# A Strassen SwiGLU stage in a fixed order: VectorE one product behind ScalarE, pair ends inside the next pair, two products in a PSUM bank of their own

## The chip, the cores and the metric

One core of a Trainium2 chip runs the whole layer. Times are device microseconds of that core for one execution; the kernel before takes 1094.98 us, the median of three runs (1094.83 to 1096.09).

## The reference

A bidirectional encoder layer on x (1 x 512 x 1024, float32): a half-step SwiGLU feed-forward net, a token mixer (a Fourier branch and multi-head latent attention, gated and summed), a second half-step SwiGLU net and a final norm. Each sub-layer starts with an RMS norm with a shift and a scale from the conditioning vector. The change lies in the second feed-forward net:

```python
def swiglu(h, w_gate, w_up, w_down):
    return (jax.nn.silu(h @ w_gate) * (h @ w_up)) @ w_down

h = modulate(rms_norm(x, ffn2_norm[l]), sh3, sc3)
x = x + 0.5 * g3[:, None, :] * swiglu(h, ffn2_w_gate[l], ffn2_w_up[l], ffn2_w_down[l])
```

D_MODEL is 1024, D_FF 2816, that is 22 hidden tiles of 128 rows.

## The kernel before

Activations lie channel-major: 128 channels by 512 tokens. Float32 operands are split in two parts in the matmul's own format: `hi` is a cast on ScalarE (L94 for weights, L108 for activations), `lo` a subtraction on VectorE (L95, L108) of `hi` from the raw tile. Three matmuls, `hi*hi`, `hi*lo` and `lo*hi` (L103 to L105), make one product of 128 channels. So every weight tile costs a load on SP's queue, a cast and a subtraction before TensorE can use it.

The second feed-forward net (`ffn_pairs`) works on pairs of hidden tiles. The first pair is computed plainly, into four banks (`out`). The other ten are Strassen pairs (class `Pair`): with the two hidden tiles, two halves of the channels and two halves of the tokens as the two-by-two blocks, each of the two weights (gate, up) needs seven products of 128 x 256 for each 512 channels, named after the block of h they take: "21", "11", "t1", "t2", "t3", "t4" and "22". A product is four chunks of three matmuls, 12 in all, of 256 columns. `Pair.run` writes out the 14 products with the sums, silus and multiplies around them; the loops go over u = 0 (gate) and u = 1 (up). In it

- `R1[u]` is a bank with "21" in its lower half and "11", later "t2", "t3" and "t4" added on, in its upper half; `R2[u]` takes "t1" and "22". All come from six banks in turn (`pbank()`); a pool `aux` of two more banks serves the norms.
- after "11", ScalarE copies the upper half to E1 (L451) and VectorE adds the lower half to it (L452).
- `release()` takes the next item off `feed.todo`: a cast and a subtraction of a weight tile that a later product needs, ending in `feed.load`, which issues the next load on SP (and, for the sum of two weight blocks, a second load on POOL's queue that adds in memory, L405). VectorE makes the other sums of blocks (L419, L420). There are six buffers each for `hi` and `lo`, five for raw tiles.
- at the end of a pair come the two hidden tiles: `second` and `s`, each a cast and a subtraction, `s` last, after the last product.

The pairs come in parts of 3, 3, 3 and 2 pairs, the plain pair being in the first part; after each part but the last, eight down projections of 128 x 512 use its hidden tiles, the last two in the order `second`, `s` (L562 adds the result to x). The first Strassen pair also has the two hidden tiles of the plain pair to finish (`aside`, L517 and L518). Inside `manual_schedule` every engine runs its instructions in the order in which the code issues them; what waits for what follows from the tiles and, in PSUM, from whole banks.

Of the kernel before, what the change touches and what calls it, by code (L numbers as in the profile page):

```python
# [10 lines left out]
F32 = mybir.dt.float32  # L11
# [49 lines left out]
def encoder_layer(ctx: ExitStack, tc: tile.TileContext, a: dict):  # L61
# [284 lines left out]
    class Feed:  # L346
# [3 lines left out]
        def __init__(self, ahead, sums_ahead):  # L350
            self.todo, self.raws, self.doubled = [], [], []
            self.ahead, self.sums_ahead = ahead, sums_ahead
# [10 lines left out]
        def release(self):  # L363
            if self.todo:
                self.todo.pop(0)()

    class Unit:
# [12 lines left out]
        def make(self):  # L380
            self.w = split(self.raw, self.n * len(self.src))
            self.feed.load(1)

    class Pair:


        def __init__(self, feed, ws, i):
            self.feed, self.ws, self.i = feed, ws, i
            self.sums, self.first, self.a1, self.s31, self.s24 = [], [], [], [], []
            self.E1, self.E2, self.R1, self.R2, self.summed = [], [], [], [], [False, False]  # L390
            for u in range(2):
                feed.doubled.append(lambda u=u: self.load_sum(u))
                feed.raws.append(lambda u=u: self.load_first(u))
                feed.todo.append(lambda u=u: self.a1.append(split(self.first[u], D)))
            feed.raws.append(self.load_last)
            for u in range(2):
                feed.todo.append(lambda u=u: self.s31.append(split(self.sums[u], D)))
                feed.todo.append(lambda u=u: self.make_s24(u))
# [24 lines left out]
        def make_s24(self, u):  # L423
            self.sum(u)
            self.s24.append(split(self.first[u], D))
            self.feed.load(1, 1)

        def make_a22(self):
            self.a22 = split(self.last, D)
            self.feed.load(1)  # L430
# [6 lines left out]
        def run(self, following=None, aside=()):  # L437

            aside = list(aside)
            V, A, release = nc.vector, nc.scalar, self.feed.release  # L440
            lo, hi = slice(0, HALF), slice(HALF, S)
            for u in range(2):
                R1 = pbank()
                self.R1.append(R1)
                self.product(R1[:, lo], self.a1[u], 1, "21", True)
                if aside:
                    aside.pop(0)()
                self.product(R1[:, hi], self.a1[u], 0, "11", True)
                E1 = tmp.tile([P, S], F32, tag=("sg", "t")[u], name=nm("E1"))
                self.E1.append(E1)  # L450
                A.copy(E1[:, lo], R1[:, hi])  # L451
                V.tensor_add(E1[:, lo], R1[:, lo], E1[:, lo])  # L452
                if u == 0:
                    A.activation(E1[:, lo], E1[:, lo], AF.Silu)
                release()
            g, up = self.E1
            for u in range(2):
                R2 = pbank()
                self.R2.append(R2)
                self.product(R2[:, lo], self.s31[u], 1, "t1", True)  # L460
                if u == 0:
                    V.tensor_mul(g[:, lo], up[:, lo], g[:, lo])
                self.product(self.R1[u][:, hi], self.s24[u], 0, "t2", False)
                A.copy(self.E1[u][:, hi], self.R1[u][:, hi])
                if u == 0 and following is not None:
                    following.sum(0)
            for u in range(2):
                self.product(self.R1[u][:, hi], self.s31[u], 0, "t3", False)
                E2 = tmp.tile([P, HALF], F32, tag=("sq", "ssum")[u], name=nm("E2"))
                self.E2.append(E2)  # L470
                A.copy(E2, self.R1[u][:, hi])
                V.tensor_add(E2, self.R2[u][:, lo], E2)
                if u == 0:
                    A.activation(E2, E2, AF.Silu, scale=-1.0)
                release()

            sg = slot32()[:, 0]
            self.product(self.R1[0][:, hi], self.a22, 0, "t4", False)
            V.scalar_tensor_tensor(sg[:, hi], self.E2[1], -1.0, self.E2[0], op0=ALU.mult, op1=ALU.mult)
            A.activation(sg[:, lo], self.R1[0][:, hi], AF.Silu, scale=-1.0)  # L480
            if following is not None:
                following.sum(1)
            self.product(self.R1[1][:, hi], self.a22, 1, "t4", False)
            V.scalar_tensor_tensor(sg[:, lo], self.R1[1][:, hi], -1.0, sg[:, lo], op0=ALU.mult, op1=ALU.mult)
            release()
            self.product(self.R2[0][:, lo], self.s24[0], 1, "22", False)
            V.tensor_add(g[:, hi], self.R2[0][:, lo], g[:, hi])
            A.activation(g[:, hi], g[:, hi], AF.Silu)
            second = slot()
            split_to(second[:, 0], second[:, 1], sg)  # L490
            release()
            self.product(self.R2[1][:, lo], self.s24[1], 1, "22", False)
# [4 lines left out]
            release()  # L497
            return [s, second]

    def ffn_pairs(ws, wd, gk, early, whole, after):  # L500
# [43 lines left out]
        following = next(pairs)  # L544
        with tc.manual_schedule(engines={E.DVE, E.Activation, E.PE, E.SP, E.Pool}):
            for pi, nk in enumerate(PARTS):
                last = pi == len(PARTS) - 1
                for n in range(1 if pi == 0 else 0, nk // 2):
                    pr, following = following, next(pairs, None)
                    got = pr.run(following if n + 1 < nk // 2 else None,  # L550
                                 [lambda j=j: hidden(*out[2 * j:2 * j + 2]) for j in range(2)] if pr is early else ())
# [653 lines left out]
```

## Time and profile before

| | |
|---|---|
| median of three runs | 1094.98 us (1094.83 to 1096.09) |
| profiled execution, its own time | 1094.74 us |
| its span, first to last instruction | 1093.0 us |
| TensorE busy | 1056.8 us, 97% |
| VectorE busy | 697.7 us, 64% |
| ScalarE busy | 453.8 us, 42% |
| stage of the Strassen pairs and their down projections | about 740 to 1058 us of the span |

PE is TensorE, PEld its weight loads, DVE VectorE, ACT ScalarE, POOL GpSimd, SP the queue that issues most loads. L103 is line 103 of the kernel; the helpers that all stages use have one line each, so tiles tell more than lines. Matmuls overlap, and their ends are modelled: a difference between two starts is safer than an idle time. A wait is put down to the instruction that ended last before it.

### The profile page before, as it was taken

The page shows a single profiled execution, that of the slowest core. Times are in us where ns is not written, and L with a number is a line of the kernel's source. Part 1 is how long each engine was busy: PE and PEld are TensorE (multiplying, and loading weights), DVE is VectorE, ACT ScalarE, POOL GpSimd, SP SyncE. Part 2 cuts the span into 40 slices and gives each one's busy share as a digit, 9 for nine tenths or more (in the row PEclk, how much of TensorE's full clock was granted, in tenths as well). Part 3 has the DMA queues.
Part 4 walks back from the last instruction along what each step waited for, and adds up shares of the span by engine and source line. Part 5 has one row for each costly group of instructions (what it writes and reads, how often), then busy time and mean ns, then how long its engine had stood idle before and what let it go on. Part 6 is the DMA issues. An engine that isn't in the chain of part 4 may idle for free.

```text
span 1093.0 us, 15644 instructions
## 1 busy us (share of the span) xinstructions
PE 1056.8 (97%) x6040; PEld 924.5 (85%) x6040; DVE 697.7 (64%) x1201; ACT 453.8 (42%) x761; POOL 104.4 (10%) x122
## 2 busy tenths in 40 slices
PE   5999999999999999999999989998999999999996
PEld 3888888888888998888888878998889888998996
DVE  6976645862563689752167767797656756665665
ACT  5532222222222444442267664365424533552454
POOL 1000000000000001000145444001000000000000
PEclk9999999999999999999999999999999999999998
DMA  9885642762473156541121124617625663573112
GB/s 360 328 316 162 232 146 87 224 216 80 143 242 97 59 199 219 176 142 39 39 66 52 58 96 128 210 40 203 195 73 159 145 211 84 157 171 110 60 38 78
DMA packets 60044, 159.61 MB, mean 146 GB/s; under 512 B 6129, under 2 KB 9841, under 8 KB 59970
## 3 DMA queue, kind: packets, MB, share of 16 engines
q1 hardware_dynamic: 55250, 143.08, 39.5%
q0 software_dynamic: 4144, 15.01, 6.5%
q8 instruction: 47, 0.77, 0.3%
q10 hardware_dynamic: 576, 0.52, 0.1%
q14 instruction: 27, 0.22, 0.1%
HBM read 154.40 MB, written 4.19 MB: 145 GB/s over the span
## 4 chain that ended last, share of the span: by engine, by line
PE 78%; DVE 8%; ACT 5%; issue 4%; DMA 2%; POOL 2%; SPq 0%; POOLq 0%; DVEq 0%; ACTq 0%
PE ps_mm L103 24%; PE ps_mm L104 24%; PE ps_mm L105 23%; PE ps_mm L590 3%; DVE lo L95 2%; ACT hi L94 2%; ACT f L108 2%; PE ps_mm L978 1%; PE ps_aux L970 1%; POOL yb L1055 1%; DMA raw<-in_wg 1%; DMA g<-in_xtok 1%; DMA g<-in_wg 1%; DVE f L108 1%; PE ps_aux L160 1%
## 5 line engine op out<-in xcount | busy, mean ns | idle before, releaser
L104 PE MATMUL ps_mm<-f,hi 128*128 128x512 f32 (+1 forms) x1120 | 408.3, 365 | 0.7 <-DVE f L108 0.7
L103 PE MATMUL ps_mm<-f,hi 128*128 128x512 f32 (+1 forms) x1120 | 408.2, 366 | 0.0
L105 PE MATMUL ps_mm<-f,lo 128*128 128x512 f32 (+1 forms) x1120 | 407.3, 364 | 0.0
L94 ACT CAST hi<-raw 128x1024 fp32r<-128x1024 f32 (+4 forms) x217 | 198.2, 916 | 363.7 <-PE ps_mm L104 283.8
L95 DVE TENSOR_TENSOR lo<-raw,hi 128x1024 fp32r<-128x1024 f32 (+3 forms) x205 | 225.4, 1101 | 140.4 <-ACT hi L94 138.7
L104 PEld LDWEIGHTS ps_mm<-f,hi 128*128 128x128 f32 x1120 | 211.2, 189 | 34.8 <-DVE f L108 1.6
L103 PEld LDWEIGHTS ps_mm<-f,hi 128*128 128x128 f32 x1120 | 210.6, 189 | 34.4 <-ACT f L108 1.7
L105 PEld LDWEIGHTS ps_mm<-f,lo 128*128 128x128 f32 x1120 | 211.0, 189 | 33.2
L103 PE MATMUL ps_mm<-b,hi 128*128 128x256 f32 x624 | 178.1, 286 | 10.4 <-DVE E L452 10.4
L104 PE MATMUL ps_mm<-b,hi 128*128 128x256 f32 x624 | 177.3, 284 | 0.0
L105 PE MATMUL ps_mm<-b,lo 128*128 128x256 f32 x624 | 177.1, 284 | 0.0
L103 PEld LDWEIGHTS ps_mm<-b,hi 128*128 128x128 f32 x624 | 120.1, 193 | 12.4 <-DVE E L452 12.0
L104 PEld LDWEIGHTS ps_mm<-b,hi 128*128 128x128 f32 x624 | 120.3, 193 | 0.1
L105 PEld LDWEIGHTS ps_mm<-b,lo 128*128 128x128 f32 x624 | 120.3, 193 | 0.0
L133 DVE SCALAR_TENSOR_TENSOR raw<-raw,g 128x1024 f32<-128x1024 f32 x56 | 68.3, 1221 | 32.5 <-DMA raw<-in_ada_w 32.2
L152 POOL TENSOR_TENSOR r<-ms,nhalf 128x2 f32<-128x2 f32 x10 | 9.5, 956 | 398.6 <-DVE ms L150 398.6
L248 DVE TENSOR_TENSOR sg<-ps_mm,sg 128x512 f32<-128x512 f32 x22 | 15.1, 690 | 50.6 <-PE ps_mm L105 50.4
L562 DVE SCALAR_TENSOR_TENSOR g<-ps_mm,gate,g 128x512 f32<-128x512 f32 x24 | 18.0, 749 | 37.7 <-PE ps_mm L105 37.7
L95 DVE TENSOR_TENSOR lo<-g,hi 128x1024 fp32r<-128x1024 f32 (+1 forms) x28 | 32.0, 1144 | 2.0 <-ACT hi L94 1.8
L94 ACT CAST hi<-g 128x1024 fp32r<-128x1024 f32 (+1 forms) x28 | 27.7, 988 | 13.3 <-PE ps_mm L104 11.6
L958 ACT ACTIVATE g<-ps_mm,st 128x512 f32<-128x512 f32 x32 | 22.1, 691 | 19.5 <-DVE st L957 17.2
L590 PE MATMUL ps_mm<-f,hi 128*128 128x512 f32 x96 | 26.3, 413 | 0.7 <-ACT f L210 0.7
(190 smaller groups left out, 1041.9 us busy)
## 6 DMA issues: line engine op xcount, KB each, us to landing
raw<-in_ada_w SPq DMA_DIRECT2D x56, 512.0 KB, 4.3
raw<-in_wd SPq DMA_DIRECT2D x48, 384.0 KB, 3.6
raw<-in_wu SPq DMA_DIRECT2D x35, 512.0 KB, 4.1
raw<-in_wg SPq DMA_DIRECT2D x31, 512.0 KB, 4.3
raw<-in_win SPq DMA_DIRECT2D x21, 512.0 KB, 3.5
g<-in_ada_w SPq DMA_DIRECT2D x16, 512.0 KB, 9.3
g<-in_wg SPq DMA_DIRECT2D x10, 512.0 KB, 5.0
g<-in_wg POOLq DMA_DIRECT2D x10, 512.0 KB, 6.3
```

The lines of the kernel that those rows point to most:

```text
L94: nc.scalar.copy(hi[:, :n], raw[:, :n])
L95: engine.tensor_sub(lo[:, :n], raw[:, :n], hi[:, :n].bitcast(F32))
L103: nc.tensor.matmul(out, lhsT=lh, rhs=rh, start=first, stop=False, skip_group_check=onto)
L104: nc.tensor.matmul(out, lhsT=lh, rhs=rl, start=False, stop=False, skip_group_check=onto)
L105: nc.tensor.matmul(out, lhsT=ll, rhs=rh, start=False, stop=last, skip_group_check=onto)
L108: return nc.scalar.copy(hi, src), engine.tensor_sub(lo, src, hi.bitcast(F32))
L133: nc.vector.scalar_tensor_tensor(raw, raw, 1.0, cb.rearrange("p c t -> p (c t)"), op0=ALU.mult, op1=ALU.mult, accum_out=mod[:, j:j + 1])
L160: nc.tensor.matmul(R[:, lo:lo + HALF], lhsT=ones, rhs=dg, start=True, stop=True)
L248: nc.vector.tensor_mul(sg, pu, sg)
L562: nc.vector.scalar_tensor_tensor(xs(m), po, gate[gk][:, m:m + 1], xs(m), op0=ALU.mult, op1=ALU.add)
L590: nc.tensor.matmul(out[i], lhsT=w[:, i * P:(i + 1) * P], rhs=h1[c][:, part], start=c == 0 and w is wh and part == 0, stop=c == NC - 1 and ...
L958: nc.scalar.activation(pr, sc, AF.Exp, bias=st[:, c:c + 1], accum_out=st[:, 4 + c:5 + c])
```

## The change

1. **A bank for the two "21" products.** `Q` comes from the `aux` banks; "21" of the gate goes to its lower, "21" of the up weight to its upper half. `R1[u]` keeps its upper half alone.
2. **Subtractions one product behind their casts.** `Feed.cut` issues the cast and queues the subtraction (and the load behind it) in `feed.low`; `cast()` takes the next cast, `rest()` the next subtraction, and `run` has both written in at fixed places. The `lo` tile of a new weight thus comes later than its `hi`.
3. **Pair ends inside the next pair.** A pair that has a follower in its part returns `end` (the last add, the multiply and the cast of hidden tile `first`) and `low` (its subtraction). The next pair runs them after its first and second product. A pair without a follower runs them itself, with no prefetch cast between.
4. The silus, sums, copies and `aside` steps are set into new places between the products; `aside` comes after the second and the fourth product instead of after the first and the third.

The core of the diff:

```diff
+        def cast(self):
+            if self.todo:
+                self.todo.pop(0)()
+        def rest(self):
+            if self.low:
+                self.low.pop(0)()
+        def cut(self, raw, n, then=lambda: None):
...
+            nc.scalar.copy(hi[:, :n], raw[:, :n])
+            def low():
+                nc.vector.tensor_sub(lo[:, :n], raw[:, :n], hi[:, :n].bitcast(F32))
+                then()
+            self.low.append(low)
+            return hi, lo
...
-            self.s24.append(split(self.first[u], D))
-            self.feed.load(1, 1)
+            self.s24.append(self.feed.cut(self.first[u], D, lambda: self.feed.load(1, 1)))
...
-        def run(self, following=None, aside=()):
+        def run(self, following, late=(), aside=()):
...
+            Q = pbank("aux", 2)
+            R1, R2 = [pbank() for _ in range(2)], []
...
+            self.product(Q[:, lo], self.a1[0], 1, "21", True)
+            late_step()
+            self.product(R1[0][:, hi], self.a1[0], 0, "11", True)
+            A.copy(g[:, lo], R1[0][:, hi])
+            feed.cast()
+            late_step()
+            if late_given:
+                feed.rest()
+            aside_step()
+            self.product(Q[:, hi], self.a1[1], 1, "21", True)
+            V.tensor_add(g[:, lo], Q[:, lo], g[:, lo])
+            feed.rest()
+            self.product(R1[1][:, hi], self.a1[1], 0, "11", True)
+            A.copy(up[:, lo], R1[1][:, hi])
+            A.activation(g[:, lo], g[:, lo], AF.Silu)
+            feed.cast()
+            aside_step()
+            R2.append(pbank())
+            self.product(R2[0][:, lo], self.s31[0], 1, "t1", True)
...
+            self.product(R1[0][:, hi], self.s31[0], 0, "t3", False)
+            A.copy(E2[0], R1[0][:, hi])
+            feed.cast()
+            self.product(R1[1][:, hi], self.s31[1], 0, "t3", False)
+            A.copy(E2[1], R1[1][:, hi])
+            feed.cast()
+            V.tensor_add(E2[0], R2[0][:, lo], E2[0])
+            feed.rest()
...
-            V.tensor_add(up[:, hi], self.R2[1][:, lo], up[:, hi])
-            V.tensor_mul(g[:, hi], up[:, hi], g[:, hi])
-            s = slot()
-            split_to(s[:, 0], s[:, 1], g)
-            release()
-            return [s, second]
+            def end():
+                V.tensor_add(up[:, hi], R2[1][:, lo], up[:, hi])
+                V.tensor_mul(g[:, hi], up[:, hi], g[:, hi])
+                A.copy(first[:, 0], g)
+            def low():
+                V.tensor_sub(first[:, 1], g, first[:, 0].bitcast(F32))
+            if following is None:
+                end()
+                low()
+                feed.rest()
+                feed.release()
+                return [first, second], ()
+            return [first, second], (end, low)
```

How it moves the instructions, at three places. Names of tiles carry their numbers; `b_1134` is block "t2" of h, `b_1132` block "t1", `b_1077` block "21" and `b_1071` block "11".

**TensorE in the second pair of the second part, from "t1" to "t2" of the gate weight**, with what an instruction waits for. Before, the target `ps_mm_1289` is R1 of the gate:

```order
L103 MATMUL ps_mm_1298_7612<-b_1132_6504,hi_1274_7454 128x256
L104 MATMUL ps_mm_1298_7612<-b_1133_6505,hi_1274_7454 128x256
L105 MATMUL ps_mm_1298_7612<-b_1132_6504,lo_1275_7455 128x256
L103 MATMUL ps_mm_1289_7545<-b_1134_6509,hi_1277_7488 128x256 [waits DVE_49]
L104 MATMUL ps_mm_1289_7545<-b_1135_6510,hi_1277_7488 128x256
L105 MATMUL ps_mm_1289_7545<-b_1134_6509,lo_1278_7489 128x256
```

Now the target is `ps_mm_1291`, again R1 of the gate:

```order
L103 MATMUL ps_mm_1302_7614<-b_1132_6504,hi_1277_7453 128x256
L104 MATMUL ps_mm_1302_7614<-b_1133_6505,hi_1277_7453 128x256
L105 MATMUL ps_mm_1302_7614<-b_1132_6504,lo_1278_7454 128x256
L103 MATMUL ps_mm_1291_7539<-b_1134_6509,hi_1280_7489 128x256 [waits Activation_49]
L104 MATMUL ps_mm_1291_7539<-b_1135_6510,hi_1280_7489 128x256
L105 MATMUL ps_mm_1291_7539<-b_1134_6509,lo_1281_7490 128x256 [waits DVE_49]
```

The matmul that opens "t2" waited for VectorE and now waits for ScalarE; the third one, which takes the low part of the weight, now has a wait for VectorE. Three products earlier, "21" of the up weight begins in the upper half of the new bank (`ps_aux_1290`), without a wait at its first matmul:

```order
L103 MATMUL ps_mm_1291_7539<-b_1071_6048,hi_1269_7362 128x256
L104 MATMUL ps_mm_1291_7539<-b_1072_6049,hi_1269_7362 128x256
L105 MATMUL ps_mm_1291_7539<-b_1071_6048,lo_1270_7363 128x256
L103 MATMUL ps_aux_1290_7538<-b_1077_6070,hi_1275_7437 128x256
L104 MATMUL ps_aux_1290_7538<-b_1078_6071,hi_1275_7437 128x256
```

**ScalarE where the same pair begins.** Before, E1_1260 is the last hidden tile of the pair ahead, E1_1290 the first of this one, `hi` a weight:

```order
L488 ACTIVATE E1_1260_7322<-E1_1260_7322 128x256
L108 CAST f_1281_7512<-g_1276_7458 128x512
L94 CAST hi_1282_7515<-g_1196_6837 128x1024
L108 CAST f_1284_7533<-E1_1260_7322 128x512
L94 CAST hi_1285_7536<-raw_1236_7136 128x1024
L451 COPY E1_1290_7570<-ps_mm_1289_7545 128x256
L454 ACTIVATE E1_1290_7570<-E1_1290_7570 128x256
L94 CAST hi_1291_7574<-raw_1249_7236 128x1024
```

Now (E1_1264 and E1_1293):

```order
L379 CAST hi_1282_7505<-g_1204_6871 128x1024
L532 CAST f_1286_7516<-g_1279_7458 128x512
L534 ACTIVATE E1_1264_7302<-E1_1264_7302 128x256
L379 CAST hi_1288_7533<-raw_1238_7138 128x1024
L543 CAST f_1287_7517<-E1_1264_7302 128x512
L478 COPY E1_1293_7541<-ps_mm_1291_7539 128x256
L379 CAST hi_1295_7571<-raw_1251_7238 128x1024
L488 COPY E1_1294_7542<-ps_mm_1292_7540 128x256
```

The last hidden tile's cast (`f_1284`, now `f_1287`) was followed by a weight's cast and then by the copy of "11"; now the copy follows it at once, and the weight's cast stands before it.

**ScalarE where the first Strassen pair begins.** `ps_mm_1128` is a bank of the plain pair, `b` are blocks of h. Before:

```order
L94 CAST hi_1149_6544<-raw_1140_6523 128x1024
L517 ACT_TABLE_LOAD
L517 ACTIVATE sg_1164_6594<-ps_mm_1128_6307 128x512
L94 CAST hi_1151_6548<-g_1045_5894 128x1024
L108 CAST b_1134_6509<-w_1046_5897 128x1024
L108 CAST b_1136_6514<-w_1048_5899 128x1024
L108 CAST b_1138_6519<-w_1047_5898 128x1024
L94 CAST hi_1153_6554<-raw_1141_6525 128x1024
L108 CAST f_1165_6597<-sg_1164_6594 128x512
L451 COPY E1_1166_6612<-ps_mm_1163_6581 128x256
```

Now:

```order
L379 CAST hi_1149_6544<-raw_1140_6523 128x1024
L379 CAST hi_1151_6548<-g_1045_5894 128x1024
L108 CAST b_1134_6509<-w_1046_5897 128x1024
L108 CAST b_1136_6514<-w_1048_5899 128x1024
L108 CAST b_1138_6519<-w_1047_5898 128x1024
L478 COPY E1_1166_6584<-ps_mm_1164_6582 128x256
L379 CAST hi_1153_6554<-raw_1141_6525 128x1024
L379 CAST hi_1168_6611<-raw_1142_6527 128x1024
L573 ACT_TABLE_LOAD
L573 ACTIVATE sg_1170_6614<-ps_mm_1128_6307 128x512
```

The table load and the silu of the plain pair's first hidden tile stood ahead of the casts of the blocks of h and now stand behind two weight casts that follow them.

## Rows read from the trace of the kernel before

**Rows 1.** Page, part 1: busy time, share of the span, instructions of each engine.

```profile
PE 1056.8 (97%) x6040; PEld 924.5 (85%) x6040; DVE 697.7 (64%) x1201; ACT 453.8 (42%) x761; POOL 104.4 (10%) x122
```

**Rows 2.** Waits (who waited for whom: us, times, longest), 742 to 1058, and after 760.

```profile
PE ps_mm L103 <- DVE E L452: 10.4, 8, 1.8
...
DVE raw L419 <- DMA g<-in_wg: 1.7, 1, 1.7
...
PE ps_mm L104 <- DVE f L108: 0.7, 3, 0.2
...
PE ps_mm L103 <- DVE E L452: 7.4, 6, 1.3
```

**Rows 3.** Windows: stretch and us, busy (xinstructions) of PE, PEld, DVE, ACT, POOL, clock, DMA, GB/s.

```profile
787.80:821.27 33.47, 33.24 (x147) 26.97 (x145) 18.21 (x22) 9.39 (x11) 0.00 (x0) 1.00 0.36 122
821.27:885.03 63.76, 61.24 (x506) 60.68 (x505) 42.50 (x63) 31.10 (x55) 5.17 (x6) 1.00 0.65 167
...
1015.66:1057.61 41.95, 40.69 (x338) 40.48 (x337) 27.60 (x40) 20.12 (x34) 0.00 (x0) 1.00 0.16 51
```

**Rows 4.** Timeline of PE around one wait: start, us, what [idle before <-releaser].

```profile
848.38 0.28 PE L104 MATMUL ps_mm<-b,hi 128*128 128x256 f32 x1
848.50 0.28 PE L105 MATMUL ps_mm<-b,lo 128*128 128x256 f32 x1
850.04 0.38 PE L103 MATMUL ps_mm<-b,hi 128*128 128x256 f32 x1 [1.26 <-DVE E L452]
850.26 0.28 PE L104 MATMUL ps_mm<-b,hi 128*128 128x256 f32 x1
```

**Rows 5.** Timeline of ACT, then of DVE, around the same wait.

```profile
847.35 1.05 ACT L94 CAST hi<-raw 128x1024 fp32r<-128x1024 f32 x1
848.29 0.36 ACT L451 COPY E<-ps_mm 128x256 f32<-128x256 f32 x1
...
848.42 1.23 DVE L95 TENSOR_TENSOR lo<-raw,hi 128x1024 fp32r<-128x1024 f32 x1 [0.26 <-ACT hi L94]
849.57 0.42 DVE L452 TENSOR_TENSOR E<-ps_mm,E 128x256 f32<-128x256 f32 x1
```

**Rows 6.** Timeline of PE, then of DVE, at the end of the last pair of the first part.

```profile
790.77 0.39 PE L104 MATMUL ps_mm<-f,hi 128*128 128x512 f32 x1
791.00 0.39 PE L105 MATMUL ps_mm<-f,lo 128*128 128x512 f32 x1
791.39 0.50 PE L103 MATMUL ps_mm<-f,hi 128*128 128x512 f32 x1
792.12 0.50 PE L104 MATMUL ps_mm<-f,hi 128*128 128x512 f32 x1 [0.23 <-DVE f L108]
...
788.93 0.96 DVE L95 TENSOR_TENSOR lo<-raw,hi 128x768 fp32r<-128x768 f32 x1
789.81 0.42 DVE L493 TENSOR_TENSOR E<-ps_mm,E 128x256 f32<-128x256 f32 x1
...
791.37 0.69 DVE L108 TENSOR_TENSOR f<-E,f 128x512 fp32r<-128x512 f32 x1 [0.69 <-ACT f L108]
```

**Rows 7.** Timeline of PE in the first Strassen pair.

```profile
748.10 0.28 PE L105 MATMUL ps_mm<-b,lo 128*128 128x256 f32 x1
749.55 0.39 PE L103 MATMUL ps_mm<-b,hi 128*128 128x256 f32 x1 [1.17 <-DVE E L452]
...
754.50 0.38 PE L103 MATMUL ps_mm<-b,hi 128*128 128x256 f32 x1 [1.82 <-DVE E L452]
```

**Rows 8.** Timeline of ACT at the start of the first Strassen pair.

```profile
737.12 1.28 ACT L517 ACT_TABLE_LOAD   x1
738.41 0.60 ACT L517 ACTIVATE sg<-ps_mm 128x512 f32<-128x512 f32 x1
...
746.25 1.05 ACT L94 CAST hi<-raw 128x1024 fp32r<-128x1024 f32 x1 [3.46 <-DVE raw L420]
```

**Rows 9.** Windows, columns as in rows 3: the stretch at a lower granted clock.

```profile
755.80:759.20 3.40, 3.40 (x18) 3.40 (x17) 1.70 (x4) 0.56 (x2) 0.00 (x0) 0.50 1.05 220
```

More of the change, by code (lines that the diff above doesn't have):

```diff
@@ L457, in run @@
[L457 to L475, printed above, removed]
@@ new lines, in run @@
+            self.product(R2[0][:, lo], self.s31[0], 1, "t1", True)
+            V.tensor_add(up[:, lo], Q[:, hi], up[:, lo])
+            V.tensor_mul(g[:, lo], up[:, lo], g[:, lo])
+            feed.rest()
+            self.product(R1[0][:, hi], self.s24[0], 0, "t2", False)
+            A.copy(g[:, hi], R1[0][:, hi])
+            if following is not None:
+                following.sum(0)
+            R2.append(pbank())
+            self.product(R2[1][:, lo], self.s31[1], 1, "t1", True)
+            self.product(R1[1][:, hi], self.s24[1], 0, "t2", False)
@@ new lines, in run @@
+            A.copy(up[:, hi], R1[1][:, hi])
+            E2 = [tmp.tile([P, HALF], F32, tag=t, name=nm("E2")) for t in ("sq", "ssum")]
+            self.product(R1[0][:, hi], self.s31[0], 0, "t3", False)
[6 more added lines that the diff above has]
+            feed.rest()
+            sg = slot32()[:, 0]
@@ new lines, in run @@
+            feed.rest()
+            second, first = slot(), slot()
+            self.product(R2[1][:, lo], self.s24[1], 1, "22", False)
+            A.copy(second[:, 0], sg)
+            V.tensor_add(g[:, hi], R2[0][:, lo], g[:, hi])
+            A.activation(g[:, hi], g[:, hi], AF.Silu)
+            if following is not None:
+                feed.cast()
+                feed.rest()
+            V.tensor_sub(second[:, 1], sg, second[:, 0].bitcast(F32))
+            def end():
+                V.tensor_add(up[:, hi], R2[1][:, lo], up[:, hi])
+                V.tensor_mul(g[:, hi], up[:, hi], g[:, hi])
+                A.copy(first[:, 0], g)
@@ L543, in ffn_pairs @@
         pairs = iter(pairs)
-        following = next(pairs)
+        following, late = next(pairs), ()
         with tc.manual_schedule(engines={E.DVE, E.Activation, E.PE, E.SP, E.Pool}):
@@ L549, in ffn_pairs @@
                     pr, following = following, next(pairs, None)
-                    got = pr.run(following if n + 1 < nk // 2 else None,
-                                 [lambda j=j: hidden(*out[2 * j:2 * j + 2]) for j in range(2)] if pr is early else ())
+                    got, late = pr.run(following if n + 1 < nk // 2 else None, late,
+                                       [lambda j=j: hidden(*out[2 * j:2 * j + 2]) for j in range(2)]
+                                       if pr is early else ())
                     act += got
```

67 lines of the change are left out of this document (31 added, 36 removed).

## Prediction

> **What bounds the kernel now.** I read the busy shares first, then the waits of TensorE in the stage that the diff touches (740 to 1058 us), then that stage cut into stretches, then the instructions around one wait of each kind. TensorE is busy 97% of the span [rows 1], so only time in which it starts nothing can be won. The waits of TensorE hold two kinds: 10.4 us in 8 waits for VectorE's add at L452, 7.4 us of it in the six after 760 us, and three small ones for the low half of the last hidden tile (L108) [rows 2].
>
> The stretches give the same loss without any model of where a matmul ends. Matmuls of 256 columns start 0.12 us apart (848.38, 848.50) [rows 4]; a pair has 14 products of 12, so three pairs should take 504 x 0.12 = 60.48 us, and the stretch from 821.27 takes 63.76 [rows 3]: 3.28 too much, for two waits (a like stretch of 63.69 us follows). The last two pairs take 41.95 for 336 x 0.12 = 40.32: 1.63 too much, for one wait. A down projection of 144 matmuls at 0.227 should take 32.7 and takes 33.47 [rows 3]: 0.78 too much, three times.
>
> What is the long wait? Product "t2" of the first weight adds into the upper half of bank R1; the lower half of the same bank holds "21", which L452 has yet to read. The matmul could have started at 848.62 and starts at 850.04, right after L452 ends at 849.99 [rows 4, 5]. L452 is late because VectorE is in order: the pair before has left its last cast on ScalarE, a prefetch cast behind it (847.35), then the copy that L452 reads (848.29), and on VectorE a subtraction of 1.23 us (848.42) ahead of the add.
>
> **The change, part by part.** No instruction is added or dropped; SP's and POOL's queues keep their order row for row. What moves is as follows.
>
> *Own bank for the two "21" products.* "t2" no longer shares a bank with what VectorE reads; its first matmul now waits for ScalarE's copy of "11". Even at the old time that copy ended at 848.29 + 0.36 = 848.65, against 848.62 wanted [rows 4, 5]: 0.03 us of wait instead of 1.42. In the new order no prefetch cast lies between the pair's last cast and the copy, which brings it some 0.9 us forward, so I take the wait as gone. One such wait costs 1.54 - 0.12 = 1.42 us, and the matmul behind it starts 0.22 instead of 0.12 later [rows 4]: 1.52 in all, which is 0.26 more than the idle time shown. Six waits: 7.4 + 6 x 0.26 = 9.0 us [rows 2]. From the stretches it is 1.63 each, or 9.8 us. I take 9.3; 9.0 and 9.8 are the ends. What is late next: the subtractions, now issued one product after their cast. The one at 848.42 ends at 849.65 [rows 5] and its reader, the second "t2", would come 10.08 us into the pair, at 841.42 + 10.08 = 851.50: 1.8 us to spare, so the delay costs nothing. Without that cover it would cost up to 1.23 us per product.
>
> The Trainium skill ("PSUM — Partial Sum Buffer", Terms, the entry on the bank) says that TensorE writing and VectorE reading one bank in the same partitions at once is an error, so a program has to keep them apart; the new bank again holds two products, and by this rule the wait could only change its place: the sum would then not be the 9.3 us gained above but the loss of rival 1. The trace agrees that the program keeps them apart by waits: the 1.42 us at "t2" is one.
>
> *Pair ends.* At the last pair of a part the prefetch no longer stands between the end and its casts. There TensorE waits for the first hidden tile: the matmul on its high half starts 0.39 us after the one before it, instead of 0.23 (791.39), that on its low half 0.73 (792.12) [rows 6]: 0.66 in all and 0.78 by the stretch. On VectorE a subtraction of 0.96 us (788.93) stood ahead of the last add and multiply (789.81); without it the low half, ready at 791.37 + 0.69 = 792.06, comes about 0.88 us sooner, at 791.18, and the undisturbed matmul would want it at 791.39 - 0.16 + 0.23 = 791.46. The high half is cast before that and needed 0.23 us earlier, so it is in time too: 3 waits x 0.66 to 0.78, I take 2.2 us; 0 and 2.3 are the ends. In other pairs the end goes into the next pair's first two products, where its reader is a down projection at least a pair away.
>
> *The first Strassen pair.* This one does not gain. Its four first products run from 741.02 to 746.78 (748.10 + 0.12 - 1.44) [rows 7]. "t1" then needs the bank that ScalarE's silu of the first hidden tile frees, and that silu, with the load of its table, moves from 737.12 to behind two casts. The first of these is released by VectorE at 746.25 as before; then two casts of 0.94 (847.35 to 848.29 [rows 5]), the load of 1.28 and the silu of 0.60 bring its end to 750.01 [rows 8]. TensorE starts nothing for 3.3 us, where it now idles 1.17 (749.55) and 1.82 (754.50) [rows 7], 0.16 more each in start times. The second "t2" comes at 750.05 + 0.10 + 3 x 1.44 = 754.47, as now. Behind it I add 0.1 us for a copy that waits for the second hidden tile's cast. The ends: -0.5 and +1.0.
>
> After today's second wait the granted clock is at 0.50, that is 1.2 GHz, for 3.4 us [rows 9], and of the 18 matmuls that touch this stretch some 16 start in it, for 28 at 0.12 us: 12 x 0.12 = 1.4 us lost. With one idle stretch of 3.3 us I expect the same once more; without a stretch at 1.2 GHz 1.4 us are gained, with a second one as much is lost.
>
> **Sum.** -9.3 - 2.2 + 0.1 = -11.4 us. The profiled execution took 1094.74 us (span 1093.0) and would take 1083.3; the median of the runs lies 0.24 above it, so the forecast is 1083.6.
>
> **Rivals.**
> 1. *The wait moves into the new bank (slower).* "21" of the second weight goes into the half beside "21" of the first. If its first matmul had to wait for VectorE's read of the other half, it would stand still at 841.42 + 2.88 = 844.30 until the add, which ended at 849.99 [rows 5]: 5.69 us instead of 1.42, 4.27 more in six pairs, so 25.6 us more: 1120.6 us. Against it: in the built order that matmul waits for nothing and the add stands behind it, so that VectorE waits until 841.42 + 4.32 = 845.74, before it is free anyway. It decides from 2.88 us into the pair: 3%.
> 2. *ScalarE becomes late.* Where "t3" and "t4" take turns on two banks, a copy of 0.36 us and a cast of 1.05 [rows 5] fill the 1.44 us between two products. If the casts start late, TensorE waits at "t4" and gives back up to 1.4 us per pair; six pairs return the 9.0 us to 1092.6, half of that is 1088. ScalarE is busy 31.10 of 63.76 us [rows 3], so it can catch up: 12%.
> 3. *The change does not do what it says.* If VectorE, or a load that now starts one product later, sets the pace of "t2" whichever bank is used, the six waits stay and only the pair ends gain: about 1092.8. The one wait for a load on VectorE is 1.7 us, in the first pair [rows 2]. 5%, called no change.
> 4. The forecast, both kinds of waits gone: 80%.
>
> **How the numbers follow.** A measurement of this kernel tells some 0.2% (2.2 us) from no change. Faster by more than that: the forecast and rival 2, 0.92. Within it: rival 3, 0.05. Slower: rival 1, 0.03. The low end of the range is the forecast with the upper ends of both gains (0.6) and no stretch at 1.2 GHz (1.4) and a little of the first pair (0.3): 1081.3. The high end has the pair ends kept (2.2) and the first pair at +1.0 (0.9 more): 1086.7. That also takes in a second stretch at 1.2 GHz, or rival 2 in two or three pairs.
>
> **What would show it.** Right: no wait of TensorE for the add of "21"; three-pair stretches of about 60.5 us; down projections of about 32.7; one idle stretch of about 3.3 us in the first Strassen pair, released by ScalarE's silu, and one low-clock stretch near it. Wrong in a step: waits of "t2" or "t4" for a ScalarE copy (rival 2), waits at the second "21" (rival 1), or waits for low halves (the subtractions have become late). The forecast is wrong if three pairs take over 62 us, or if the first pair loses over 5 us.

## The result, and the profile after

The changed kernel takes 1083.58 us (median of four runs, 1082.30 to 1084.41), the kernel before 1094.99 in the same comparison: ratio 0.9893, 95% interval 0.9876 to 0.9910. The forecast was 1083.6, within 1081.3 to 1086.7. The time is right. The experiments will show that one of the reasons given for it was not needed for it.

The profiled execution took 1082.98 us, its span 1081.2, against 1094.74 and 1093.0 before. Busy shares of the kernel after (page, part 1) answer to [rows 1]:

```profile
PE 1053.3 (97%) x6040; PEld 924.2 (85%) x6040; DVE 698.3 (65%) x1201; ACT 456.4 (42%) x761; POOL 104.7 (10%) x122
```

Every engine is busy as long as before within 0.6%: it is idle time of TensorE that went. The waits of the kernel after (735 to 1062 us: who waited for whom, us in total, times, longest) hold one of TensorE's in the Strassen stage, where [rows 2] had eight of 10.4 us and three of 0.7:

```profile
PE ps_mm L103 <- ACT sg L573: 3.2, 1, 3.2
```

The stretches of the kernel after, columns as in [rows 3]: a down projection, three pairs, the last two pairs, the stretch at the lower clock, the first pair's 8 us from 749, and the end of the span:

```profile
785.83:818.50 32.67, 32.67 (x147) 27.04 (x145) 18.05 (x22) 8.61 (x10) 0.00 (x0) 1.00 0.35 120
818.50:878.97 60.47, 60.47 (x506) 60.47 (x504) 42.51 (x63) 32.38 (x56) 5.19 (x6) 1.00 0.70 180
1004.78:1045.09 40.31, 40.31 (x337) 40.31 (x336) 27.99 (x41) 20.95 (x36) 0.00 (x0) 1.00 0.18 53
...
749.37:752.78 3.41, 2.85 (x13) 2.85 (x14) 2.19 (x4) 1.83 (x5) 2.15 (x3) 0.50 1.06 235
...
749.00:757.00 8.00, 7.07 (x48) 7.07 (x49) 4.90 (x8) 4.50 (x9) 2.58 (x3) 0.79 1.05 232
...
1045.09:1081.20 36.11, 26.55 (x206) 25.00 (x204) 21.49 (x56) 15.37 (x34) 1.39 (x2) 0.90 0.17 59
```

Set against [rows 3], three pairs lose 63.76 - 60.47 = 3.29 us and again 3.22, the last two 1.64, each of the three down projections 0.80. The first part's pairs lose 1.76 (740.06 to 787.80 before, 739.85 to 785.83 now), of which 1.5 is the wait of its second pair, and the start 0.2. The end (from 1045.09, before from 1057.61) is 36.11 instead of 35.39, 0.72 longer. The sum is -0.2 - 1.76 - 3.29 - 3.22 - 1.64 - 2.40 + 0.72 = -11.8 us, the whole difference of the spans. (In the kernel before, one matmul of the end, 0.12 us, ran at 1047.41 among those of the last pairs: x338 there, x337 now. For equal work the last two pairs lose 1.52, and the end is 0.60 longer.) 60.47 us for 504 matmuls is 0.12 each: no time without a start is left in these pairs.

The timeline of the kernel after at three places (start, us, engine, what; in brackets the idle time before and what ended it): the first Strassen pair on TensorE and ScalarE, one later pair that begins at 838.65 on VectorE, and VectorE at the first part's end, where the down projection begins at 785.83:

```profile
746.45 0.28 PE L105 MATMUL ps_mm<-b,lo 128*128 128x256 f32 x1
749.93 0.58 PE L103 MATMUL ps_mm<-b,hi 128*128 128x256 f32 x1 [3.20 <-ACT sg L573]
750.31 0.41 PE L104 MATMUL ps_mm<-b,hi 128*128 128x256 f32 x1
750.52 0.41 PE L105 MATMUL ps_mm<-b,lo 128*128 128x256 f32 x1
...
745.97 1.99 ACT L379 CAST hi<-raw 128x1024 fp32r<-128x1024 f32 x2 [1.71 <-DVE raw L440]
747.98 1.28 ACT L573 ACT_TABLE_LOAD   x1
749.28 0.60 ACT L573 ACTIVATE sg<-ps_mm 128x512 f32<-128x512 f32 x1
...
844.19 0.42 DVE L485 TENSOR_TENSOR E<-ps_aux,E 128x256 f32<-128x256 f32 x1
...
845.66 0.42 DVE L494 TENSOR_TENSOR E<-ps_aux,E 128x256 f32<-128x256 f32 x1
...
786.47 0.42 DVE L541 TENSOR_TENSOR E<-ps_mm,E 128x256 f32<-128x256 f32 x1
```

The first pair does what was forecast: TensorE stands still for 3.2 us until the silu, which follows two casts and a table load, ends at 749.88 (forecast 750.01). The second place raises a doubt. "t2" of the first weight starts 5 x 1.44 = 7.20 us into the pair, at 845.85, and VectorE has finished reading "21" at 844.61. It is 1.24 us early, so the wait would be gone **whichever bank "21" lies in**. At the third place the last add starts 0.64 us after the down projection; in [rows 6] it started at 789.81 - 787.80 = 2.01.

### The profile page after: what moved, and what is told of

Its sections match the earlier page's. It is cut to its first block, busy times and chain, and to the rows that moved or that the text cites. A ratio compares the mean times of both kernels' runs of the same rounds, so it can differ in the third digit from the quotient of the medians.

```text
span 1081.2 us, 15646 instructions
## 1 busy us (share of the span) xinstructions
PE 1053.3 (97%) x6040; PEld 924.2 (85%) x6040; DVE 698.3 (65%) x1201; ACT 456.4 (42%) x761; POOL 104.7 (10%) x122
## 4 chain that ended last, share of the span: by engine, by line
PE 90%; DVE 4%; ACT 2%; issue 2%; POOL 1%; DMA 1%; SPq 0%; POOLq 0%; DVEq 0%; ACTq 0%
PE ps_mm L103 27%; PE ps_mm L104 27%; PE ps_mm L105 27%; PE ps_mm L647 3%; PE ps_mm L1035 1%; PE ps_aux L1027 1%; PE ps_aux L105 1%; PE ps_aux L104 1%; PE ps_aux L103 1%; DMA g<-in_xtok 1%; DVE b L108 1%; ACT f L108 1%; PE ps_aux L160 1%; PE ps_aux L145 0%; ACT g L1015 0%
## 5 line engine op out<-in xcount | busy, mean ns | idle before, releaser
L94 ACT CAST hi<-raw 128x1024 fp32r<-128x1024 f32 (+4 forms) x139 | 121.8, 882 | 290.0 <-PE ps_mm L104 250.3
L95 DVE TENSOR_TENSOR lo<-raw,hi 128x1024 fp32r<-128x1024 f32 (+3 forms) x127 | 136.6, 1078 | 100.8 <-ACT hi L94 99.7
L103 PE MATMUL ps_mm<-b,hi 128*128 128x256 f32 x544 | 154.2, 284 | 3.2 <-ACT sg L573 3.2
L104 PE MATMUL ps_mm<-b,hi 128*128 128x256 f32 x544 | 154.5, 284 | 0.0
L105 PE MATMUL ps_mm<-b,lo 128*128 128x256 f32 x544 | 154.4, 284 | 0.0
L379 ACT CAST hi<-raw 128x1024 fp32r<-128x1024 f32 (+1 forms) x78 | 76.5, 981 | 76.9 <-PE ps_mm L104 37.3
L103 PEld LDWEIGHTS ps_mm<-b,hi 128*128 128x128 f32 x544 | 104.9, 193 | 3.4 <-ACT sg L573 3.4
L104 PEld LDWEIGHTS ps_mm<-b,hi 128*128 128x128 f32 x544 | 105.0, 193 | 0.0
L105 PEld LDWEIGHTS ps_mm<-b,lo 128*128 128x128 f32 x544 | 105.0, 193 | 0.0
L382 DVE TENSOR_TENSOR lo<-raw,hi 128x1024 fp32r<-128x1024 f32 (+1 forms) x78 | 88.6, 1139 | 16.3 <-ACT hi L379 15.5
L379 ACT CAST hi<-g 128x1024 fp32r<-128x1024 f32 x20 | 21.1, 1054 | 14.7 <-PE ps_mm L104 14.7
```

The costliest lines, as they stand in the source:

```text
L94: nc.scalar.copy(hi[:, :n], raw[:, :n])
L95: engine.tensor_sub(lo[:, :n], raw[:, :n], hi[:, :n].bitcast(F32))
L103: nc.tensor.matmul(out, lhsT=lh, rhs=rh, start=first, stop=False, skip_group_check=onto)
L104: nc.tensor.matmul(out, lhsT=lh, rhs=rl, start=False, stop=False, skip_group_check=onto)
L105: nc.tensor.matmul(out, lhsT=ll, rhs=rh, start=False, stop=last, skip_group_check=onto)
L379: nc.scalar.copy(hi[:, :n], raw[:, :n])
```

## Is it the bank or the order?

Theory A, the prediction's: the bank of its own removes the six waits at "t2". Theory B: the order does, by having VectorE read "21" earlier. Three kernels take the two apart, beside one on the first pair (below).

**The order without the bank.**

```diff
-            Q = pbank("aux", 2)
-            self.product(Q[:, lo], self.a1[0], 1, "21", True)
+            self.product(R1[0][:, lo], self.a1[0], 1, "21", True)
-            self.product(Q[:, hi], self.a1[1], 1, "21", True)
+            self.product(R1[1][:, lo], self.a1[1], 1, "21", True)
...
```

> The change without the bank of its own: both "21" products go into the lower halves of R1 again, everything else in the new order. Theory A (the prediction's: the own bank removes the six waits): the six waits of about 1.5 us for VectorE's add are back, 9.0 to 9.8 us, so 1092.6 to 1093.4 us, and three-pair stretches of about 63.7 us. Theory B (the order removes them: in the trace after, the add of the first "21" runs 844.19 to 844.61 in a pair that starts at 838.66, and "t2" starts at 838.66 + 7.20 = 845.86, 1.25 us behind it; the second add ends at 846.08, "t2" of the second weight starts at 848.74): no wait in the six pairs, three-pair stretches of 60.5 us. Only in the first Strassen pair the second "t2" (755.59 in the trace after) would have to wait for the add that ends at 756.64, about 1.1 us: 1084.7 us.

Measured: 1083.68 us (1083.19 to 1084.62), ratio to before 0.9897 (0.9883 to 0.9912). That is the change's own time. Its windows of three pairs and of the stretch at the lower clock, and its timeline on VectorE (down to the add that reads "21" of the first weight, L484) and on TensorE ("t2" of the first weight) in a pair that begins at 840.82:

```profile
820.67:881.14 60.47, 60.47 (x506) 60.47 (x504) 42.48 (x63) 32.37 (x56) 5.17 (x6) 1.00 0.66 174
...
749.40:756.20 6.80, 5.39 (x25) 5.39 (x26) 3.54 (x5) 4.45 (x8) 2.58 (x3) 0.53 1.03 264
```

```profile
844.61 0.69 DVE L545 TENSOR_TENSOR f<-E,f 128x512 fp32r<-128x512 f32 x1 [0.69 <-ACT f L542]
845.22 1.22 DVE L382 TENSOR_TENSOR lo<-raw,hi 128x1024 fp32r<-128x1024 f32 x1
846.35 0.41 DVE L484 TENSOR_TENSOR E<-ps_mm,E 128x256 f32<-128x256 f32 x1
...
848.02 0.28 PE L103 MATMUL ps_mm<-b,hi 128*128 128x256 f32 x1
```

The add ends at 846.76 and "t2" starts on time at 848.02, in the very bank that the add has read. Theory A's 1092.6 does not come; the order alone gives the gain. What it does to VectorE shows against the kernel before, in the pair of [rows 5], which begins at 841.42:

```profile
843.82 0.69 DVE L108 TENSOR_TENSOR f<-g,f 128x512 fp32r<-128x512 f32 x1 [0.99 <-ACT f L108]
844.77 1.23 DVE L95 TENSOR_TENSOR lo<-g,hi 128x1024 fp32r<-128x1024 f32 x1 [0.26 <-ACT hi L94]
...
847.47 0.69 DVE L108 TENSOR_TENSOR f<-E,f 128x512 fp32r<-128x512 f32 x1 [0.69 <-ACT f L108]
```

A weight's subtraction stands right ahead of the add in both kernels (848.42 in [rows 5], 845.22 here). But before, VectorE stood idle for ScalarE four times between the pair's start and the add, 0.99 + 0.26 + 0.69 + 0.26 = 2.2 us; here it does so once, for 0.69. The add ends 5.94 us into the pair in place of 8.57. Of these 2.6 us 1.5 are idle time; most of the rest is a weight's subtraction that filled the pair's first 1.1 us and now ends 0.2 us into it. (The 1.1 us that theory B expected in the first pair did not show in this profile; there TensorE ran at the lower clock for most of 6.8 us and came later itself.)

**The bank without the order**, each "21" in a bank of its own:

```diff
-                R1 = pbank()
+                R1, q = pbank(), pbank("aux", 2)[:, lo]
...
-                self.product(R1[:, lo], self.a1[u], 1, "21", True)
+                self.product(q, self.a1[u], 1, "21", True)
...
-                V.tensor_add(E1[:, lo], R1[:, lo], E1[:, lo])
+                V.tensor_add(E1[:, lo], q, E1[:, lo])
```

> The kernel before, its order kept, but each "21" product in a bank of its own. Theory A: the six waits go, "t2" follows ScalarE's copy within 0.03 to 0.4 us: three-pair stretches of 60.5 to 61.3 us, the first pair loses its two waits too (1.3 to 3.3 us), the down projections still take 33.47: 1095.0 - 9.3 - 2 = about 1083.7, at least under 1087. Theory B (only the order does it): the waits stay, 1095.

Measured: 1086.14 us (1085.34 to 1086.97), ratio 0.9919 (0.9904 to 0.9934). A window of three pairs, and the timeline around "t2" of the first weight (TensorE, then ScalarE's copy and VectorE's add):

```profile
818.54:879.98 61.44, 61.34 (x506) 60.72 (x504) 42.40 (x63) 31.05 (x55) 5.18 (x6) 1.00 0.62 164
```

```profile
845.99 0.39 PE L103 MATMUL ps_mm<-b,hi 128*128 128x256 f32 x1
...
845.57 0.36 ACT L451 COPY E<-ps_mm 128x256 f32<-128x256 f32 x1
...
846.84 0.42 DVE L452 TENSOR_TENSOR E<-ps_aux,E 128x256 f32<-128x256 f32 x1
```

Here the add is as late as before (it ends 8.57 us into the pair in both), and "t2" starts 0.85 us ahead of it, 0.06 after the copy. So the mechanism of the prediction exists: a bank of its own for each product takes the wait away too. 61.44 leaves 0.97 us in slower starts, the largest 0.26, and the down projections stay at 33.47. Against what was expected, the first Strassen pair keeps its idle time: one wait of 2.45 us, for ScalarE's copy, stands in place of the two of [rows 7]. Bank and order are two remedies for one wait, each enough by itself.

**The bank of the change without the order**, both "21" in two halves of one bank:

```diff
+            Q = pbank("aux", 2)
             for u in range(2):
-                R1 = pbank()
+                R1, q = pbank(), Q[:, (lo, hi)[u]]
...
```

> The kernel before, its order kept, with the bank of the change: both "21" products in two halves of one bank of their own. Theory A in its plain form (any bank apart from R1 will do): about 1084 to 1087. Theory B with rival 1 of the prediction (the second "21" stands still until the add of the first, 5.69 us in place of 1.42 in six pairs): slower than before by about 25.6 us, 1120.6, or some more if the first pairs of the parts wait too; three-pair stretches of 72 us or more.

Measured: 1144.41 us (two runs), ratio 1.0451 (1.0428 to 1.0474). Its waits of TensorE in the stage, and the timeline of the second "21" with the add that it waits for:

```profile
PE ps_aux L103 <- DVE E L453: 45.1, 10, 5.6
```

```profile
861.97 0.42 DVE L453 TENSOR_TENSOR E<-ps_aux,E 128x256 f32<-128x256 f32 x1
...
862.44 0.58 PE L103 MATMUL ps_aux<-b,hi 128*128 128x256 f32 x1 [5.58 <-DVE E L453]
```

This is rival 1 of the prediction, its place and its price right (5.69 forecast, 5.58 in these pairs, the matmul starting right behind the add). It cost more than 25.6 us: the first pair of each later part waits as well (2.05 us, three times), the first Strassen pair once (5.48), and the mean granted clock fell to 0.972. The waits are 45.1 - 10.4 = 34.7 us more than before; the other 15 of the 49.6 us lost (1144.41 - 1094.83, the median of the kernel before in the same comparison) go in the main with starts 0.21 us apart behind the long waits (granted clock 0.50 from 862 to 866). The Trainium skill ("PSUM — Partial Sum Buffer", Terms, the entry on the bank) states that a write of TensorE and a read of VectorE on one bank in the same partitions at once are an error. The trace agrees in so far as the program keeps the two apart, with 5.58 us of waiting; the error itself no run here shows. So the bank of the change is no help on its own: shared by two products, it needs the order.

## Which part of the order?

**Subtractions at their casts, no bank.** The order as in the first kernel above, but each low half is subtracted right behind its cast:

```diff
-            self.low.append(low)
+            low()
             return hi, lo
```

> The new order with neither of two things: the "21" products share R1 again, and every weight's low-half subtraction is issued right behind its cast instead of one product later; the place of the pair ends and all else stay new. Theory B1 (it is the late subtraction that takes VectorE out of the way: 1.22 us each, seven a pair, and a VectorE that reaches one right after its cast was issued stands up to the cast's 1.05 us before it): the six waits are back, at 1.5 us or more each, three-pair stretches of 63.5 us or more, the down projections start late again: 1083.7 + 9 + 2 = 1094.7 or more. Theory B2 (the rest of the order, pair ends queued into the next pair above all, does it): no such waits, about 1084 to 1085.

Measured: 1122.27 us (1121.20 to 1124.04), ratio 1.0251 (1.0236 to 1.0267): 38.6 us above the same order with late subtractions. The waits of TensorE in the six pairs:

```profile
PE ps_mm L103 <- DVE E L484: 18.6, 6, 3.1
```

A window of three pairs, and the timeline of VectorE ahead of one wait with the matmuls on both sides of it:

```profile
825.87:897.89 72.02, 65.56 (x505) 64.80 (x504) 42.36 (x62) 31.77 (x54) 5.18 (x6) 0.93 0.59 151
```

```profile
850.03 1.23 DVE L382 TENSOR_TENSOR lo<-raw,hi 128x1024 fp32r<-128x1024 f32 x1 [1.61 <-ACT hi L379]
851.17 0.69 DVE L537 TENSOR_TENSOR f<-g,f 128x512 fp32r<-128x512 f32 x1
...
854.56 1.23 DVE L382 TENSOR_TENSOR lo<-raw,hi 128x1024 fp32r<-128x1024 f32 x1 [1.90 <-ACT hi L379]
855.70 0.68 DVE L545 TENSOR_TENSOR f<-E,f 128x512 fp32r<-128x512 f32 x1
856.30 0.42 DVE L484 TENSOR_TENSOR E<-ps_mm,E 128x256 f32<-128x256 f32 x1
...
853.48 0.28 PE L105 MATMUL ps_mm<-b,lo 128*128 128x256 f32 x1
856.87 0.55 PE L103 MATMUL ps_mm<-b,hi 128*128 128x256 f32 x1 [3.10 <-DVE E L484]
```

This is how the six waits come back. VectorE twice stands idle (1.61, 1.90 us) in front of a subtraction whose cast ScalarE has yet to make, while the gate's work behind it, which ScalarE itself needs for its next casts, is ready. The two in-order engines hold each other up, and the add of "21" ends at 856.72. The kernel with the order alone, one product behind, waits in front of no weight's subtraction in its pair. Each wait costs 856.87 - 853.48 - 0.12 = 3.27 us in start times, two of them 6.5 of the 72.02 - 60.47 = 11.55. Of the rest 0.8 lies in smaller waits, and some 4.2 in starts about 0.21 apart behind the two waits (granted clock 0.50 from 857 to 861; 0.93 over the whole stretch).

**Subtractions at their casts, with the bank** (the same edit on the change):

> The change, its bank kept, but every subtraction issued right behind its cast. Theory: either the bank or the late subtraction alone keeps TensorE from waiting in the six pairs, so the long waits stay away; three-pair stretches within 0.5 to 2 us of 60.5. The down projections, whose gain the prediction put down to the prefetch moved from between a pair's end and its casts, tell whether it is that (then 32.7 still) or VectorE freed of subtractions (then 33.3 to 33.5 again, 2 us in all). 1083.6 if both gains stay, 1085.6 to 1090 if not.

Measured: 1092.02 us (ten runs, 1089.78 to 1094.10), ratio 0.9975 (0.9965 to 0.9984). Windows of three pairs and of a down projection:

```profile
820.42:882.62 62.20, 61.72 (x505) 60.77 (x504) 42.36 (x62) 31.43 (x54) 5.18 (x6) 1.00 0.67 174
786.77:820.42 33.65, 33.22 (x147) 26.96 (x145) 18.44 (x24) 9.23 (x11) 0.00 (x0) 1.00 0.29 101
```

The long waits stay away, as theory has it, but small ones (the longest 0.22 us idle) put 1.73 us back on three pairs, and the down projections start late again: 33.65. Of the change's 11.4 us 2.6 are left, less than was expected (1085.6 to 1090). So the new order needs its late subtractions, with the bank or without. That the delay alone would do in the old order does not follow: there each subtraction stands right behind its cast too, but ahead of the add VectorE waits only twice for such a cast, 0.26 us each time, where it waits 1.61 and 1.90 above. The old order with late subtractions, and the new places (point 4) by themselves, were not run.

**Ends in their own pair, no bank**: `end()`, `low()` and the `rest()` behind them are called where a pair stops, for every pair.

> The new order without the bank and without the queued pair ends: the last add, multiply, cast and subtraction of a pair are issued at its own end, where they stood before. Theory B1: the queued ends do nothing, since their readers are a pair or more away: 1083.7, stretches of 60.5. Theory B2: the six waits are back: 1092 or more.

Measured: 1084.51 us (1084.12 to 1084.86), ratio 0.9904 (0.9887 to 0.9920), every three pairs 60.5, every down projection 32.7. Queueing the ends into the next pair moves nothing beyond what the runs spread (0.8 us over the order alone, with overlapping intervals; this profile does show theory B's wait of 1.0 us in the first pair, ahead of which the two kernels have the same order).

**The prefetch ahead of the last pair's end** (an edit on the change):

```diff
-            if following is not None:
-                feed.cast()
-                feed.rest()
+            feed.cast()
+            feed.rest()
...
                 feed.rest()
-                feed.release()
                 return [first, second], ()
```

> The change, but in the last pair of each part the prefetch cast stands again ahead of the last gate and its casts, as it did before and does in the other pairs; its subtraction stays one product late. The prediction's theory of the pair ends (the prefetch between a pair's end and its casts makes the hidden tile late): the down projections start late again, 33.3 to 33.5 us in place of 32.67, 2.2 us in all: 1085.8. Rival, after the run with subtractions at their casts (33.7): it is VectorE freed of subtractions that brings the tile in time, and the prefetch costs nothing: 32.67, 1083.6.

Measured: 1082.80 us (1082.58 to 1084.21), ratio 0.9895 (0.9880 to 0.9909): the rival. Its windows of the first pair's 8 us from 749 and of the first down projection, and its timeline on VectorE around the start of that down projection (785.42):

```profile
749.00:757.00 8.00, 6.44 (x52) 6.27 (x53) 4.30 (x7) 5.51 (x10) 2.58 (x3) 1.00 1.01 249
785.42:818.09 32.67, 32.67 (x146) 27.05 (x145) 17.67 (x22) 8.61 (x10) 0.00 (x0) 1.00 0.34 120
```

```profile
784.93 0.96 DVE L382 TENSOR_TENSOR lo<-raw,hi 128x768 fp32r<-128x768 f32 x1
785.81 0.69 DVE L537 TENSOR_TENSOR f<-g,f 128x512 fp32r<-128x512 f32 x1
786.41 0.42 DVE L540 TENSOR_TENSOR E<-ps_mm,E 128x256 f32<-128x256 f32 x1
```

The same place in the kernel before, ahead of the rows of VectorE in [rows 6]:

```profile
788.20 0.69 DVE L108 TENSOR_TENSOR f<-g,f 128x512 fp32r<-128x512 f32 x1 [0.99 <-ACT f L108]
```

Where the prefetch's cast stands does not matter. Nor does it matter that a weight's subtraction of 0.96 us (784.93) still stands ahead of the last add (786.41): it belongs to the cast before, has nothing to wait for, and lies in time in which VectorE stood idle before (0.99 us in front of 788.20). The add starts 0.99 us after the down projection, against 2.01 before.

## The first pair, and a version that beats both

**The silu ahead of the casts.** The first hidden tile's step moves right behind the first product, the second's behind "t2" of the second weight:

```diff
             late_step()
+            aside_step()
             self.product(R1[0][:, hi], self.a1[0], 0, "11", True)
...
-            aside_step()
             self.product(Q[:, hi], self.a1[1], 1, "21", True)
...
-            aside_step()
             R2.append(pbank())
...
             A.copy(up[:, hi], R1[1][:, hi])
+            aside_step()
```

> The change with the silu of the first hidden tile moved ahead of the two casts on ScalarE in the first Strassen pair (right behind the first product), and that of the second hidden tile moved behind "t2" of the second weight. Theory: the idle 3.2 us of TensorE in the first pair (749.93, 3.48 us after the matmul before) is the silu's place on ScalarE alone: it goes, 3.36 us; and if the clock falls because TensorE stood idle, its stretch at 0.50 goes too, 13 matmuls in 2.9 us in place of 1.6, another 1.3: 1083.6 - 4.7 = 1078.9. If the clock falls for another reason there: 1080.2. Rival: the casts, now behind a table load and a silu, hold a later product for as long: 1083.

Measured: 1084.83 us (1081.51 to 1085.51), ratio 0.9900 (0.9876 to 0.9925): no gain. The idle time has moved. The timeline on VectorE, ScalarE and TensorE:

```profile
756.42 0.69 DVE L439 TENSOR_TENSOR raw<-g,raw 128x512 f32<-128x512 f32 x1 [3.25 <-DMA g<-in_wg]
...
757.76 0.68 DVE L574 TENSOR_TENSOR sg<-ps_mm,sg 128x512 f32<-128x512 f32 x1
...
758.48 0.62 ACT L108 CAST f<-sg 128x512 fp32r<-128x512 f32 x1 [4.30 <-DVE sg L574]
759.00 0.36 ACT L507 COPY E<-ps_mm 128x256 f32<-128x256 f32 x1
...
759.42 0.39 PE L103 MATMUL ps_mm<-b,hi 128*128 128x256 f32 x1 [3.28 <-ACT E L507]
```

My placing of the second step put it behind a sum (L439) that waits for a load. VectorE's multiply came 3.25 us late, ScalarE's copy behind it, and TensorE stood still for that copy. **One place earlier**, behind "t2" of the first weight and so ahead of that sum:

```diff
             A.copy(g[:, hi], R1[0][:, hi])
+            aside_step()
             if following is not None:
                 following.sum(0)
...
             A.copy(up[:, hi], R1[1][:, hi])
-            aside_step()
```

> As early_silu, with the second hidden tile's silu one place earlier: behind "t2" of the first weight, and so ahead of the sum (L439) on VectorE, which waited until 756.42 for a load that the DMA queues brought late and kept the hidden tile's multiply behind it. Theory: no product of the first pair waits any more: the 3.3 us go, and with them the stretch at clock 0.50: 1084.8 - 4.7 = 1080.1 against the run before it, 1078.9 against the change. Rival: the load that comes at 756.4 is itself what the first pair waits for (through the casts of the next pair's weights), and the 3 us show up one pair later: 1083 to 1085.

Measured: 1079.39 us (1078.83 to 1080.98), ratio 0.9860 (0.9846 to 0.9875), 4.2 us under the change; the two intervals do not overlap. No product of the first pair waits for that load any more. 3.5 of the 4.0 us between the spans of the two profiles lie ahead of the first down projection. Window of the first pair, in the columns of [rows 3]:

```profile
749.00:757.00 8.00, 7.94 (x66) 7.74 (x66) 5.97 (x10) 5.71 (x12) 2.89 (x4) 1.00 1.00 248
```

66 matmuls lie in these 8 us (48 in the change's), all at the full clock.

**And the same without the bank:**

> early_silu_2 with the "21" products back in R1. What is the bank worth in an order that does not stand still in the first pair? There "t2" of the first weight starts at 741.71 + 7.20 = 748.91, and VectorE's add of "21" ends at 749.77 + 0.42 = 750.19: 1.28 us of wait, and about 0.1 for the slower matmul behind it. In the six other pairs nothing, stretches of 60.47. 1079.4 + 1.4 = 1080.8; if the clock falls after that wait, about 1.4 more: 1082.2. If the bank is worth nothing at all: 1079.4.

Measured: 1080.61 us (1078.78 to 1080.76), ratio 0.9867 (0.9851 to 0.9884). Its waits of TensorE hold the one that was expected:

```profile
PE ps_mm L103 <- DVE E L484: 1.2, 1, 1.2
```

This is what the bank is worth in the new order, as far as these runs show: 1.2 us, once, in the pair in which VectorE is still busy with the hidden tiles. The two intervals overlap, so the wait shows it and the times alone do not.

## Why the prediction was right, and where it was not

- **What bounds the kernel**: right. Nothing but TensorE's idle time was to be won, and the arithmetic on starts (0.12 us each, 60.48 for three pairs) gave the end point: 60.47.
- **Six waits, 9.3 us**: the size is right (3.29 + 3.22 + 1.52 + 1.5 = 9.5), the step's cause is not. The step that failed is "own bank for the two '21' products": it gives the bank all 9.3 us and the order none. Without the bank the time is 1083.7, the change's own. The subtractions' delay, which by the prediction "costs nothing", indeed costs nothing, but it is also a part of the order that the gain cannot do without: with neither it nor the bank the time is 1122.3. The bank would have done the work in the old order, one bank for each product; in the new order no run shows it worth more than 1.2 us. The prediction did not work out where the add would end. It ends 2.6 us earlier in its pair, and the copy ahead of it, which was to come some 0.9 us forward, comes 3.2 forward (it ends 842.69 - 838.65 = 4.04 us into the pair, before 848.65 - 841.42 = 7.23). One reading was off by little: the 1.63 of the last two pairs holds the 0.12 of a matmul that is not theirs, so that 1.52 was the price there.
- **Pair ends, 2.2 us**: 2.40 came. That the last add was late was right, that the prefetch had to go from between the end and its casts was wrong: with it back the down projections still take 32.67. And a subtraction ahead of the add is not enough to make it late: one stands there in that kernel too, in time in which VectorE had stood idle, which the prediction did not count.
- **The first pair, +0.1**: one idle stretch of 3.2 us released by the silu, one stretch at the lower clock, as said; from the budget -0.3, within the ends.
- **Rival 1** did not come, for the reason given (the add ends before it is needed); taking the order away made it come at its price. **Rivals 2 and 3** did not come: TensorE waits nowhere for a copy in the six pairs.
- **The end, +0.7 us**, was not in the sum. 0.12 of it is the matmul named above. The rest does not come with the order or the bank: with the same instructions the end takes 35.54 us in the kernel with the order alone (from 1047.26) and 35.59 in the one with the silu one place earlier (from 1041.61), but 36.12 in the one with the prefetch first (from 1044.68). What makes it one or the other was not tried.
- **The close agreement**, 1083.58 for 1083.6, is luck in two ways. The kernel's four runs spread over 2.1 us, and gains of 0.2 us in each kind of wait and some 0.6 in the start and the first pair, none of them forecast, met a loss at the end and a profiled run 0.6 us under the median. And the wrong cause did no harm because another part of the same change did the work that was credited to the bank.

## What to carry to other kernels

When a matmul waits for a reader of its bank, there are two questions: must it share the bank, and why is the reader late? Here either answer was enough, and only kernels with one part each could say which one a change had used. On two in-order engines that feed each other, look at what an instruction waits for in its place in the queue. A follow-up (the low half of a split) set right behind the cast it depends on stopped everything queued after it for 1.6 to 1.9 us here; set one step behind, it waited for nothing, and could even fill time in which the engine stood idle. A second product put into a spare half of a new bank brings the same wait back unless the order keeps the reader ahead.

## What the runs showed of the hardware

The lower clock does not follow from the length of an idle stretch alone. In the same first pair an idle 1.82 us [rows 7] was followed by 3.4 us at a granted clock of 0.50 [rows 9], 1.2 GHz; in the change the clock fell within the idle 3.2 us; in the kernel with the order alone it was 0.53 over 6.8 us; and in the kernel with the prefetch first the idle stretch was there (3.19 us) and the clock stayed at 1.00 (its window from 749.00). Such a stretch costs the change 13 x (0.21 - 0.12) = 1.2 us (750.31 to 750.52 is one start to the next). The four runs of the change take longer the lower their mean granted clock is: 1082.30 us at 0.996, 1082.98 at 0.995, 1084.18 at 0.994 and 1084.41 at 0.993. That stretches like this one make that spread is likely but not shown, as only one run of a kernel has a profile. So the first part of a single profile can be off by 1 us, while the three-pair stretches behind it are 60.47 or 60.48 us in every kernel that has none of the waits.
